# A state space scan as one scan instruction on turned states, streamed in eight units, in place of 62 steps

## The chip, the cores and the metric

The kernel runs on one core of a Trainium2 chip. It is one launch of an encoder layer on two sequences. The metric is the device time of one execution in microseconds (us). A core has five engines that work at the same time from queues of their own: PE (TensorE, matmuls; PEld is its weight load), DVE (VectorE), ACT (ScalarE), POOL (GpSimd) and SP (SyncE, which issues nearly all DMAs here). Instructions of one engine run in the order of its queue; between engines they wait on semaphores. All data is fp32; gate and projection matmuls take each operand as a high and a low part (fp32r), so that one product is three matmuls.

## The reference, cut to what matters

The layer norms the input `x` (512 tokens, width 1024, two sequences), projects it by `w_in`, and has three branches: a state space branch (S5), a differential attention and a cross attention to a memory. They are gated, summed, projected, and a feed-forward network follows. The change touches the S5 branch alone:

```python
def _ssm_combine(e1, e2):
    a1, b1 = e1
    a2, b2 = e2
    return a1 * a2, a2 * b1 + b2

def _s5_scan_dir(u, lam, step, b, c):
    lam_bar = jnp.exp(lam * step[:, None])
    b_bar = ((lam_bar - 1.0) / lam)[..., None] * b
    bu = jnp.einsum('lgh,gph->lgp', u.astype(jnp.complex64), b_bar)
    a = jnp.broadcast_to(lam_bar, bu.shape)
    _, xs = lax.associative_scan(_ssm_combine, (a, bu), axis=0)
    return jnp.real(jnp.einsum('lgp,ghp->lgh', xs, c))
```

There are 32 groups (`g`) of 16 channels (`h`) and 64 complex states (`p`), and two directions over the tokens, whose outputs are summed. A gelu and a gated linear unit (glu) follow: `z * sigmoid(z @ w_glu + b_glu)`.

## The kernel before, in words

Tokens are cut into 64 chunks (`NC`) of 8 (`T`). Inside a chunk the recurrence is written out as matmuls; across chunks a state per group has to be carried on. Partitions 0 to 63 hold the states of the forward direction and 64 to 127 those of the backward one, so a state tile is 128 partitions x real or imaginary x 32 groups x 2 sequences x 64 chunks.

`s5_gen` (from L1468) is a Python generator. Whenever the program calls `next(s5)`, the next part of the branch is written into the instruction stream; between the calls stands other work. In order it does this:

- constants: from lambda and step it works out powers of the complex decay (L1489 to L1563), small DVE instructions of 128x32;
- `input_weights(o)` for each of four blocks `o` of eight groups (L1615): six DVE products of 128x1024 (L1609 to L1611), transposes on PE (L1623), copies by ACT (L1624), kept in SBUF (`wb`);
- `output_weights(o)` (L1638): six more such products, two copies on POOL (L1640, L1641), small matmuls for the kernels inside a chunk (L1656; two at a time, with outputs at partitions 0 and 64), all stored to DRAM (`cD`, `gD5`);
- states: `u` is loaded back from DRAM into one tile (L1674); 64 matmuls of 128x128 weights and 128 columns (L1687) give each chunk's input to the state; ACT and DVE copy them into the state tile `st` (L1690, L1691);
- the scan across chunks: 62 steps of four DVE instructions on 128x128 (L1702 to L1705), a complex multiply and add;
- outputs: for each block copies of the states (L1738, L1739), 96 matmuls (three for each group, L1746 to L1748), copies by ACT, stores to `yD` (L1753). The gelu stage (L501 to L512) reads `yD`, and its results `zh`, `zl` are the moving operands of the glu projections (L524).

The other work that fills the time between is `gates(n)` (L400): each gate is a projection of 48 matmuls of 128x128 by 512 columns (L66 is the line of a helper that records every matmul), with a weight tile loaded by SP (L146), cast to its high part by ACT (L134, `wh`) and its low part by DVE (L135, `wl`), two buffers of each, and a tanh on ACT (L408). `NG` says how many gates stand where: `NG[0]` before the scan, `NG[1]` less some along it, one at each of the scan's places in `SCAN` but the first, two among the outputs, and `NG[2]` after the gelu stage. That is 7, 2, 4, 2 and 3.

A scheduler gives each engine its order: it walks the program as written, simulates the engines' times, and puts an instruction on its queue when it would be ready, those written earlier first. `tc.issue_after(x)` makes instructions of `x`'s engine in the block stand behind `x` on that engine. The scan's parts are held behind the split of the last gate's weight (`last_s[1]` is the `wl` on DVE), the outputs behind the last gate's last matmul.

Pools hold the tiles in SBUF. A pool that closes gives its memory to the next, which waits for the instructions that still use it: the state tile takes the memory that the constants leave.

Of the kernel before, what the change touches and what calls it, by code (L numbers as in the profile page):

```python
# [10 lines left out]
F32 = mybir.dt.float32  # L11
# [30 lines left out]
NG = (7, 6, 3)  # L42
# [3 lines left out]
SCAN = (33, 40, 47, 53, 60)  # L46
# [26 lines left out]
def encoder(ctx: ExitStack, tc: tile.TileContext, a, out):  # L73
# [339 lines left out]
    next(s5)  # L413
    gates(NG[1] + 1 - len(SCAN))
    for i in range(len(SCAN)):
        if i:
            gates(1)
        with tc.issue_after(last_s[1].ins):
            next(s5)
    for n in (0, 1, 1):  # L420
        gates(n)
        with behind():
            next(s5)
    next(s5, None)

# [1042 lines left out]
def s5_gen(k):  # L1468
# [3 lines left out]
    st, pre, rt = ExitStack(), ExitStack(), ExitStack()  # L1472
    k.open_tags(st, su=1)
    sp = st.enter_context(tc.tile_pool(name="s5", bufs=1, reuse_waits="tile"))
    cp = rt.enter_context(tc.tile_pool(name="s5c", bufs=1, side="right", reuse_waits="tile"))
    V.memset(cp.tile([P, 64], F32, name="pad_s"), 0.0)
    k.open_tags(rt, side="right", it=3, wb=6)
# [86 lines left out]

    yield
# [48 lines left out]

    def input_weights(o):  # L1615
        res = []
        for w_ in cprod("it", by_group(b_r, o), by_group(b_i, o), by_token(qr, o), by_token(qi, o), True):
# [7 lines left out]
            res.append(t_)  # L1625
        return res

    wbs = [input_weights(o) for o in range(3)]
# [39 lines left out]
    output_weights(0)  # L1668
    output_weights(1)
    uv = k.uD.rearrange("(g h) j s c -> j h g (s c)", h=16)  # L1670
    u_ = slot("su", [P, G, NS * NC], name="u_")
    for o in range(4):
        for j in range(8):
            nc.sync.dma_start(u_[j * 16 : (j + 1) * 16, 8 * o : 8 * o + 8], uv[j, :, 8 * o : 8 * o + 8])  # L1674


    pre.close()
    ss = st.enter_context(tc.tile_pool(name="s5s", bufs=1, reuse_waits="tile"))
    st_t = ss.tile([P, 2, G, NS, NC], F32, name="st")
    PO.memset(st_t[:, :, :, :, 0:1], 0.0)  # L1680
    for o in range(4):
        for ri, w_ in enumerate(wbs[o]):
            for g4 in range(2):
                ps = aux()
                for g in range(4):
                    gg = g4 * 4 + g
                    PE.matmul(ps[:, g * P : (g + 1) * P], w_[:, gg * P : (gg + 1) * P], u_[:, 8 * o + gg, :], start=True, stop=True)  # L1687
                pv = ps.rearrange("p (q c) -> p q c", c=NC)
                dv = st_t[:, ri, 8 * o + 4 * g4 : 8 * o + 4 * g4 + 4].rearrange("p g s c -> p (g s) c")
                S.copy(dv[0:64, :, 1:NC], pv[0:64, :, 0 : NC - 1])  # L1690
                V.tensor_copy(dv[64:128, :, NC - 1 : 0 : -1], pv[64:128, :, 1:NC])  # L1691
        if o == 0:
            wbs.append(input_weights(3))
    for o in range(2, 4):
        output_weights(o)
    yield
    sv = st_t.rearrange("p r g s c -> p r (g s) c")
    l8rv, l8iv = l8r.rearrange("p r g s -> p r (g s)"), l8i.rearrange("p r g s -> p r (g s)")
    for i in range(2, NC):
# [8 lines left out]
    yield  # L1708

    rt.close()  # L1710
    k.open_tags(rt, side="right", x2=2, oc=4, ow=3, sy=2)
# [141 lines left out]
```

## Time and profile before

| what | value |
|---|---|
| runs | 1588.4 and 1587.11 us, median 1587.76 us |
| profiled execution, span from first to last instruction | 1585.2 us (no other time is given for it) |
| PE busy | 99% of the span |
| DVE, ACT, POOL busy | 74%, 40%, 35% |
| DMA moved | 237.84 MB, mean 150 GB/s |
| first and last instruction of the 62 scan steps | 148.4 to about 254 us |
| last store of the branch's output issued | 317.4 us |
| glu projection begins | 345 us |

The profile is one execution, recorded by the hardware. Busy time is the time in which at least one instruction of an engine ran. Matmuls overlap in the pipeline, so a matmul's duration is not its price: the time from one start to the next is. A group row gives line, engine, operation, output and inputs by name, shapes, count, then busy us and mean ns of one, then the engine's idle time just before such instructions and what ended it. A row of one line or tile gives the least, median and greatest duration in ns and the first and last start in us. The profiler counts an fp32 matmul as two records, each with a weight load of its own.

### The profile page before, as it was taken

The page shows a single profiled execution, that of the slowest core. Times are in us where ns is not written, and L with a number is a line of the kernel's source. Part 1 is how long each engine was busy: PE and PEld are TensorE (multiplying, and loading weights), DVE is VectorE, ACT ScalarE, POOL GpSimd, SP SyncE. Part 2 cuts the span into 40 slices and gives each one's busy share as a digit, 9 for nine tenths or more (in the row PEclk, how much of TensorE's full clock was granted, in tenths as well). Part 3 has the DMA queues.
Part 4 walks back from the last instruction along what each step waited for, and adds up shares of the span by engine and source line. Part 5 has one row for each costly group of instructions (what it writes and reads, how often), then busy time and mean ns, then how long its engine had stood idle before and what let it go on. Part 6 is the DMA issues. An engine that isn't in the chain of part 4 may idle for free. (4 is left out here: it accounts for less than half of the span.)

```text
span 1585.2 us, 21351 instructions
## 1 busy us (share of the span) xinstructions
PE 1574.0 (99%) x7738; PEld 1310.4 (83%) x7738; DVE 1170.4 (74%) x1859; ACT 631.6 (40%) x1115; POOL 549.5 (35%) x434
## 2 busy tenths in 40 slices
PE   9999999999999999999999999999999999999998
PEld 7888888888898779778888888888888888888777
DVE  7978995076774776866545669788888877988864
ACT  6644223265552455564223443333333333233323
POOL 0010000001333321300343355767777553444663
PEclk9999999999999999999999999999999999999999
DMA  9553623676763121135544422333333323885412
GB/s 363 183 170 119 212 94 116 180 266 204 269 218 113 41 100 41 47 127 174 198 140 128 137 93 93 112 107 120 120 120 125 118 84 128 306 324 184 160 61 107
DMA packets 105675, 237.84 MB, mean 150 GB/s; under 512 B 13665, under 2 KB 45409, under 8 KB 105569
## 3 DMA queue, kind: packets, MB, share of 16 engines
q1 hardware_dynamic: 104992, 236.06, 44.2%
q8 instruction: 61, 1.00, 0.3%
q14 instruction: 46, 0.37, 0.1%
q10 hardware_dynamic: 576, 0.41, 0.1%
HBM read 165.16 MB, written 71.27 MB: 149 GB/s over the span
## 5 line engine op out<-in xcount | busy, mean ns | idle before, releaser
L66 PE MATMUL bkmm<-xh,wh 128*128 128x512 f32 x640 | 255.3, 399 | 0.0
L66 PE MATMUL bkmm<-xh,wl 128*128 128x512 f32 x640 | 250.6, 392 | 0.0
L66 PE MATMUL bkmm<-xl,wh 128*128 128x512 f32 x640 | 250.1, 391 | 0.0
L66 PE MATMUL bkmm<-tl,wh 128*128 128x512 f32 (+1 forms) x621 | 241.1, 388 | 0.0
L66 PE MATMUL bkmm<-th,wl 128*128 128x512 f32 (+1 forms) x621 | 240.7, 388 | 0.0
L66 PE MATMUL bkmm<-th,wh 128*128 128x512 f32 (+1 forms) x621 | 240.7, 388 | 0.0
L134 ACT CAST wh<-wf 128x1024 fp32r<-128x1024 f32 (+2 forms) x134 | 117.6, 878 | 261.2 <-PE bkmm L66 190.4
L135 DVE TENSOR_TENSOR wl<-wf,wh 128x1024 fp32r<-128x1024 f32 (+2 forms) x134 | 147.6, 1102 | 60.5 <-ACT wh L134 55.4
L66 PE MATMUL bkmm<-th,w 128*128 128x512 f32 x432 | 140.7, 391 | 1.9 <-DVE nsq L1112 1.2
L66 PEld LDWEIGHTS bkmm<-xh,wh 128*128 128x128 f32 x640 | 120.3, 188 | 26.2 <-issue 3.4
L66 PEld LDWEIGHTS bkmm<-xh,wl 128*128 128x128 f32 x640 | 120.2, 188 | 26.2 <-issue 0.4
L66 PEld LDWEIGHTS bkmm<-xl,wh 128*128 128x128 f32 x640 | 120.4, 188 | 22.3
L66 PEld LDWEIGHTS bkmm<-th,wh 128*128 128x128 f32 x621 | 116.6, 188 | 24.0
L66 PEld LDWEIGHTS bkmm<-th,wl 128*128 128x128 f32 x621 | 116.5, 188 | 24.1 <-DVE wl L135 0.2
L66 PEld LDWEIGHTS bkmm<-tl,wh 128*128 128x128 f32 x621 | 116.6, 188 | 23.8
L1175 POOL TENSOR_TENSOR up<-up,acc 128x512 f32<-128x512 f32 x44 | 83.7, 1920 | 90.6 <-DVE up L1112 86.8
L452 POOL TENSOR_TENSOR raw<-raw 128x128 f32<-128x128 f32 x28 | 14.6, 523 | 288.9 <-DVE nb L543 231.9
L66 PEld LDWEIGHTS bkmm<-th,w 128*128 128x128 f32 x432 | 80.9, 188 | 22.1 <-DVE nsq L1112 2.1
L792 POOL TENSOR_TENSOR mg<-mg,gl 128x1024 f32<-128x1024 f32 x16 | 43.8, 2740 | 136.8 <-DVE gl L788 132.1
L66 PE MATMUL bkmm<-tl,w 128*128 128x512 f32 x216 | 84.1, 389 | 0.0
L134 ACT CAST wh<-ws 128x1024 fp32r<-128x1024 f32 x44 | 46.3, 1052 | 91.3 <-PE bkmm L66 49.7
L66 PE MATMUL bkmm<-yh,wh 128*128 128x512 f32 x192 | 76.2, 397 | 0.0
(663 smaller groups left out, 3535.4 us busy)
## 6 DMA issues: line engine op xcount, KB each, us to landing
wf<-in_w_in SPq DMA_DIRECT2D x40, 512.0 KB, 3.9
wD<-hl SPq DMA_DIRECT2D x28, 512.0 KB, 2.9
w<-wD SPq DMA_DIRECT2D x28, 512.0 KB, 4.8
gD<-gt SPq DMA_DIRECT2D x24, 512.0 KB, 2.9
gl<-gD SPq DMA_DIRECT2D x24, 512.0 KB, 3.7
wf<-in_w_fg SPq DMA_DIRECT2D x22, 512.0 KB, 3.6
wf<-in_w_fu SPq DMA_DIRECT2D x22, 512.0 KB, 3.5
aD<-ac SPq DMA_DIRECT2D x22, 512.0 KB, 2.8
```

Of the source, the lines that this page charges most:

```text
L66: return self.put(self.eng.matmul(*args, **kw))
L134: h = S.copy(hi, src)
L135: l_ = V.tensor_tensor(out=lo, in0=src, in1=hi.bitcast(F32), op=ALU.subtract)
L452: PO.tensor_tensor(out=a22, in0=a21, in1=a22, op=ALU.add)
L792: PO.tensor_tensor(out=mg[m], in0=mg[m], in1=gt, op=ALU.add)
L1175: PO.tensor_tensor(out=up, in0=up, in1=accs[s], op=ALU.mult)
```

## The change

The decay is taken apart into its size and its phase. If each state is turned back by the phase of its chunk, what is left is a real recurrence with a constant real factor, and real and imaginary parts run on their own. After it the states are turned forward again. One new DVE instruction, `tensor_tensor_scan`, does a whole real recurrence: 512 elements for four groups, two sequences and 64 chunks, where a zero in front of each sequence's first chunk stops the carry.

- New constants: `wc`, `ws` (the phase over eight tokens) and `r8` (the size), 22 small DVE instructions before the first input weights; `l8r` and `l8i` go.
- A table `tab` of the phases of 64 chunks for 32 groups, made on POOL by doubling (36 instructions of 32 to 992 elements), stored to DRAM (`tD5`).
- `input_weights` stores its result to DRAM (`bD5`) and all four blocks come before the units.
- The states, scan and outputs become eight units of four groups. `unit_in(q)` loads `u`, weights and a piece of the table; `states(q)` does 16 matmuls with half of the columns each (64 wide, 126 moving columns, at output partitions 0 and 64, those of the second half reading the chunks in reverse), turns the states (four multiplies on DVE that read PSUM, two adds on POOL) and runs two scans; `outputs(q)` turns them back (four multiplies on DVE, adds by halves on DVE and POOL) and does the 12 matmuls of four groups as before.
- `output_weights(o)` moves to the units, one every second unit. Unit `q`'s states stand with unit `q-1`'s outputs in one step of the generator.
- Gates: two before, one after each of the nine steps, four after them, three after the gelu stage.

The diff, cut:

```diff
-NG = (7, 6, 3)
+NG = (2, 4, 3)
...
-SCAN = (33, 40, 47, 53, 60)
...
     next(s5)
     gates(NG[0])
-    next(s5)
-    gates(NG[1] + 1 - len(SCAN))
-    for i in range(len(SCAN)):
-        if i:
-            gates(1)
+    for _ in range(9):
         with tc.issue_after(last_s[1].ins):
             next(s5)
-    for n in (0, 1, 1):
-        gates(n)
-        with behind():
-            next(s5)
+        gates(1)
     next(s5, None)
+    gates(NG[1])
...
+    rot = sp.tile([P, 8, G], F32, name="rot")
...
+    wc, ws, r8, ra = (rot[:, i, :] for i in range(4))
+    q1, q2 = ta[:, :G], tb[:, :G]
+    V.tensor_scalar(out=ra, in0=E, scalar1=1.0, scalar2=None, op0=ALU.add)
+    V.tensor_tensor(out=r8, in0=ra, in1=ra, op=ALU.mult)
+    V.tensor_tensor(out=ra, in0=r8, in1=r8, op=ALU.mult)
+    V.tensor_tensor(out=r8, in0=ra, in1=ra, op=ALU.mult)
+    c_, s_ = cp1, sn
+    for _ in range(3):
+        V.tensor_tensor(out=q1, in0=c_, in1=c_, op=ALU.mult)
+        V.tensor_tensor(out=q2, in0=s_, in1=s_, op=ALU.mult)
+        V.scalar_tensor_tensor(out=ws, in0=c_, scalar=2.0, in1=s_, op0=ALU.mult, op1=ALU.mult)
+        V.tensor_tensor(out=wc, in0=q1, in1=q2, op=ALU.subtract)
+        c_, s_ = wc, ws
+    V.tensor_tensor(out=q1, in0=wc, in1=wc, op=ALU.mult)
+    V.tensor_tensor(out=q2, in0=ws, in1=ws, op=ALU.mult)
+    V.tensor_tensor(out=q1, in0=q1, in1=q2, op=ALU.add)
+    V.tensor_scalar(out=q1, in0=q1, scalar1=-0.5, scalar2=1.5, op0=ALU.mult, op1=ALU.add)
+    V.tensor_tensor(out=wc, in0=wc, in1=q1, op=ALU.mult)
+    V.tensor_tensor(out=ws, in0=ws, in1=q1, op=ALU.mult)
...
-    l8r = sp.tile([P, 2, G, NS], F32, name="l8r")
-    l8i = sp.tile([P, 2, G, NS], F32, name="l8i")
-    for s in range(NS):
-        for ri in range(2):
-            S.copy(l8r[:, ri, :, s], pr[:, 8, :])
-        S.mul(l8i[:, 0, :, s], pi[:, 8, :], -1.0)
-        S.copy(l8i[:, 1, :, s], pi[:, 8, :])
...
+    bD = drp.tile([4, P, 2, 8 * P], F32, name="bD5")
...
+            nc.sync.dma_start(bD[o, :, ri], t_)
...
+    input_weights(3)
+    wt.close()
+    pre.close()
+    tD = drp.tile([8, P, 2, 4, NC], F32, name="tD5")
+    with tc.tile_pool(name="s5t", bufs=1, reuse_waits="tile") as tp:
+        tab = tp.tile([P, 2, G, NC], F32, name="tab")
+        u1, u2 = (tp.tile([P, G, NC // 2], F32, name=n_) for n_ in ("tu1", "tu2"))
+        PO.memset(tab[:, 0, :, 0:1], 1.0)
+        PO.memset(tab[:, 1, :, 0:1], 0.0)
+        for ri, w_ in enumerate((wc, ws)):
+            PO.tensor_copy(tab[:, ri, :, 1], w_)
+        n = 1
+        while n < NC - 1:
+            m = min(n, NC - 1 - n)
+            hi = [tab[:, ri, :, n : n + 1].broadcast_to([P, G, m]) for ri in range(2)]
+            lo = [tab[:, ri, :, 1 : m + 1] for ri in range(2)]
+            cmul(PO, tab[:, 0, :, n + 1 : n + 1 + m], tab[:, 1, :, n + 1 : n + 1 + m], *hi, *lo, u1[:, :, :m], u2[:, :, :m])
+            n += m
+        for q in range(8):
+            nc.sync.dma_start(tD[q], tab[:, :, 4 * q : 4 * q + 4])
+    k.open_tags(st, z5=1, uu=2, bw=2, tb=2, ow=2, oc=2, sy=2, tm=4, x2=2)
+    zt = slot("z5", [P, 2, 3, 4, NS, NC], name="zt5")
+    PO.memset(zt.rearrange("p a r g s c -> p (a r g s) c")[:, :, 0:1], 0.0)
...
+    def unit_in(q):
+        o, h4 = q // 2, q % 2
+        if h4 == 0:
+            us[o] = slot("uu", [P, 8, NS * NC], name="u_")
+            for j in range(8):
+                nc.sync.dma_start(us[o][j * 16 : (j + 1) * 16], uv[j, :, 8 * o : 8 * o + 8])
+        bw = slot("bw", [P, 2, 4 * P], name="bw")
+        nc.sync.dma_start(bw, bD[o, :, :, 512 * h4 : 512 * h4 + 512])
+        tb = slot("tb", [P, 2, 4, NC], name="tb")
+        nc.sync.dma_start(tb, tD[q])
+        ins[q] = bw, tb
+    def states(q):
+        o, h4 = q // 2, q % 2
+        bw, tb = ins[q]
+        z = zt[:, q % 2]
+        S.copy(z[:, 2, :, :, 1:], r8[:, 4 * q : 4 * q + 4].unsqueeze(2).unsqueeze(3).broadcast_to([P, 4, NS, NC - 1]))
+        bk = [aux() for _ in range(2)]
+        for g in range(4):
+            ug = us[o][:, 4 * h4 + g].rearrange("p (s c) -> p s c", s=NS)
+            for ri in range(2):
+                for hf, u_ in enumerate((ug[:, :, 0 : NC - 1], ug[:, :, NC - 1 : 0 : -1])):
+                    d_ = bk[ri][64 * hf : 64 * hf + 64, g * P : (g + 1) * P].rearrange("p (s c) -> p s c", s=NS)
+                    tc.keep_in_program_order(
+                        PE.matmul(d_[:, :, 1:], bw[:, ri, g * P + 64 * hf : g * P + 64 * hf + 64], u_, start=True, stop=True))
+        bk = [b_.rearrange("p (g s c) -> p g s c", g=4, s=NS)[:, :, :, 1:] for b_ in bk]
+        cs, sn_ = (tb[:, i, :, 1:].unsqueeze(2).broadcast_to([P, 4, NS, NC - 1]) for i in range(2))
+        for i, op in enumerate((ALU.add, ALU.subtract)):
+            t_ = slot("tm", [P, 4, NS, NC], name="tm")
+            V.tensor_tensor(out=z[:, i, :, :, 1:], in0=bk[i], in1=cs, op=ALU.mult)
+            V.tensor_tensor(out=t_[:, :, :, 1:], in0=bk[1 - i], in1=sn_, op=ALU.mult)
+            PO.tensor_tensor(out=z[:, i, :, :, 1:], in0=z[:, i, :, :, 1:], in1=t_[:, :, :, 1:], op=op)
+        for i in range(2):
+            zf = z[:, i].rearrange("p g s c -> p (g s c)")
+            V.tensor_tensor_scan(out=zf, data0=z[:, 2].rearrange("p g s c -> p (g s c)"), data1=zf, initial=0.0,
+                                 op0=ALU.mult, op1=ALU.add)
+    def outputs(q):
+        o, h4 = q // 2, q % 2
+        _, tb = ins.pop(q)
+        z = zt[:, q % 2]
+        if h4 == 0:
+            w_ = slot("ow", [P, 8, P], name="w_")
+            gv = gD[8 * o : 8 * o + 8].rearrange("g h t q -> h g (t q)")
+            for j in range(8):
+                nc.sync.dma_start(w_[j * 16 : (j + 1) * 16], gv[:, :, (7 - j) * 16 : (7 - j) * 16 + 128])
+            ys[o] = w_, slot("sy", [P, 8, P], name="y_")
+        w_, y_ = ys[o]
+        cc = slot("oc", [P, 2, 4, P], name="cc")
+        for ri in range(2):
+            nc.sync.dma_start(cc[:, ri], cD[o, ri, :, 4 * h4 : 4 * h4 + 4, 0:P])
+        x2 = slot("x2", [P, 2, 4 * NS, NC], name="x2")
+        sh = [P, 4, NS, NC]
+        cs, sn_ = (tb[:, i].unsqueeze(2).broadcast_to(sh) for i in range(2))
+        for i, op in enumerate((ALU.subtract, ALU.add)):
+            t1, t2 = (slot("tm", sh, name="tm") for _ in range(2))
+            V.tensor_tensor(out=t1, in0=z[:, i], in1=cs, op=ALU.mult)
+            V.tensor_tensor(out=t2, in0=z[:, 1 - i], in1=sn_, op=ALU.mult)
+            t1, t2 = (t_.rearrange("p g s c -> p (g s) c") for t_ in (t1, t2))
+            V.tensor_tensor(out=x2[0:64, i], in0=t1[0:64], in1=t2[0:64], op=op)
+            PO.tensor_tensor(out=x2[64:128, i, :, ::-1], in0=t1[64:128], in1=t2[64:128], op=op)
+        ps = aux()
+        for g in range(4):
+            d_ = ps[:, g * P : (g + 1) * P]
+            PE.matmul(d_, w_[:, 4 * h4 + g, :], us[o][:, 4 * h4 + g, :], start=True, stop=False)
+            for ri in range(2):
+                PE.matmul(d_, cc[:, ri, g], x2[:, ri, 2 * g : 2 * g + 2, :].rearrange("p s c -> p (s c)"), start=False, stop=(ri == 1))
+        S.copy(y_[:, 4 * h4 : 4 * h4 + 4, :].rearrange("p g c -> p (g c)"), ps)
+        if h4:
+            for j in range(8):
+                nc.sync.dma_start(yv[j, :, 8 * o : 8 * o + 8], y_[j * 16 : (j + 1) * 16])
+    unit_in(0)
...
-    for i in range(2, NC):
-        p_ = sp.tile([P, 2, G * NS], F32, tag="p_", name="p_")
-        q_ = sp.tile([P, 2, G * NS], F32, tag="q_", name="q_")
-        V.tensor_tensor(out=p_, in0=sv[:, :, :, i - 1], in1=l8rv, op=ALU.mult)
-        V.tensor_tensor(out=q_, in0=sv[:, ::-1, :, i - 1], in1=l8iv, op=ALU.mult)
-        V.tensor_tensor(out=p_, in0=p_, in1=sv[:, :, :, i], op=ALU.add)
-        V.tensor_tensor(out=sv[:, :, :, i], in0=p_, in1=q_, op=ALU.add)
-        if i in SCAN:
-            yield
...
+    for q in range(9):
+        if q % 2 == 0 and q < 8:
+            output_weights(q // 2)
+        if q + 1 < 8:
+            unit_in(q + 1)
+        if q < 8:
+            states(q)
+        if q:
+            outputs(q - 1)
+        yield
```

More of the change, by code (lines that the diff above doesn't have):

```diff
@@ L1612, in cprod @@
         return tiles
+    bD = drp.tile([4, P, 2, 8 * P], F32, name="bD5")
     def input_weights(o):
-        res = []
-        for w_ in cprod("it", by_group(b_r, o), by_group(b_i, o), by_token(qr, o), by_token(qi, o), True):
+        for ri, w_ in enumerate(cprod("it", by_group(b_r, o), by_group(b_i, o), by_token(qr, o), by_token(qi, o), True)):
             w_ = w_.rearrange("p g e h -> p (g e h)")
@@ L1624, in input_weights @@
                 S.copy(t_[:, g4 * 512 : g4 * 512 + 512], tr)
-            res.append(t_)
-        return res
-    wbs = [input_weights(o) for o in range(3)]
+            nc.sync.dma_start(bD[o, :, ri], t_)
+    for o in range(3):
+        input_weights(o)
     yield
@@ L1666, in output_weights @@
                 nc.sync.dma_start(gv[:, :, 112:128], gk[r0 + 32 : r0 + 48, :, 128:144])
-    output_weights(0)
-    output_weights(1)
-    uv = k.uD.rearrange("(g h) j s c -> j h g (s c)", h=16)
[L1671 to L1693, printed above, removed]
```

57 lines of the change are left out of this document (6 added, 51 removed).

## The prediction

> **What bounds the kernel now.** I read the page's head first, then the busy time of each engine by stage, then the matrix engine's instructions in order of time through the stretch that the change touches.
>
> ```profile
> span 1585.2 us, 21351 instructions
> PE 1574.0 (99%) x7738; PEld 1310.4 (83%) x7738; DVE 1170.4 (74%) x1859; ACT 631.6 (40%) x1115; POOL 549.5 (35%) x434
> ```
>
> A busy matmul row may hide slack, so the stages count for more. The columns are busy us and instruction counts of PE, weight load, DVE, ACT, POOL, then granted clock, DMA share, GB/s.
>
> ```profile
> 95.00:150.00 55.00, 55.00 (x374) 47.78 (x374) 42.86 (x47) 27.45 (x53) 4.92 (x5) 1.00 0.55 175
> 150.00:255.00 105.00, 105.00 (x500) 86.82 (x497) 98.59 (x259) 25.53 (x43) 0.58 (x2) 1.00 0.41 137
> 255.00:315.00 60.00, 60.00 (x364) 53.33 (x363) 9.05 (x8) 19.30 (x23) 0.00 (x0) 1.00 0.49 149
> 315.00:350.00 35.00, 35.00 (x156) 28.99 (x155) 26.03 (x48) 20.76 (x30) 0.00 (x0) 1.00 0.75 259
> ```
>
> From 95 to 350 us PE is never idle and its clock is at 1.00. The scan with its 248 small DVE instructions lies in 150:255, where DVE is busy 98.59 of 105 us, and PE runs gate projections all that time. So DVE is nearly full there and still off the path. Whether a busy PE also advances is seen from its starts (time, duration, then the instruction):
>
> ```profile
> 102.40 0.39 PE L66 MATMUL bkmm<-xh,wh 128*128 128x512 f32 x1
> 102.62 0.39 PE L66 MATMUL bkmm<-xl,wh 128*128 128x512 f32 x1
> 102.94 0.45 PE L1656 MATMUL bktr<-cxi,l 128*48 128x144 f32 x4
> 103.23 0.42 PE L1656 MATMUL bktr<-cxr,l 128*48 128x144 f32 x4
> ...
> 104.70 0.42 PE L1656 MATMUL bktr<-cxr,l 128*48 128x144 f32 x4
> 105.04 0.50 PE L66 MATMUL bkmm<-xh,wl 128*128 128x512 f32 x1
> 105.38 0.39 PE L66 MATMUL bkmm<-xh,wh 128*128 128x512 f32 x1
> ...
> 117.79 2.05 PE L1687 MATMUL bktr<-u__1192,wb 128*128 128x128 f32 x16
> 119.60 0.48 PE L66 MATMUL bkmm<-xh,wh 128*128 128x512 f32 x1
> 119.92 1.05 PE L1687 MATMUL bktr<-u__1192,wb 128*128 128x128 f32 x8
> ```
>
> Gate matmuls start every 0.227 us (the 0.39 us are overlapping lives), which makes a gate of 48 of them 10.9 us. Nothing waits between them. **The consequence**: in this stretch PE sets the end. A shorter scan gives nothing back by itself. The change can gain only what it takes off PE's own list of matmuls, and can lose what it adds to that list or whatever makes PE stand still.
>
> **The sum, PE's list first.** Against the profiled execution (span 1585.2 us; no other time of it is given) the two timed runs lie 1.9 and 3.2 us higher, the median 1587.76 lies 2.6 higher. I add 2.6 to every sum.
>
> Gates: 7+2+4+2 stand before the gelu stage now, 2+9+4 after the change, and 3 behind in both. Eighteen gates stay, at 10.9 us each; they only change places. Transposes of the input weights, kernel matmuls of L1656 and the 96 output matmuls stay in number.
>
> State matmuls: now 64 full 128x128 ones, two records each; 16 records take 1.81 us (117.79 to 119.60), so 0.113 a record, 0.226 a matmul, 14.5 us in all. After: 64 pairs, each pair filling columns 0 to 63 and 64 to 127 with 126 moving columns. A pair of half-width fp32 matmuls has a row: in L1656 a line of x4 is two matmuls with outputs at partitions 0 and 64, and 8 such lines take 2.10 us (102.94 to 105.04, the change-over at the end included). That is 0.245 us a pair net of 0.1 for that change-over, while one matmul of 144 columns by itself would need 0.25 (0.226 x 144/128). So the two halves run at the same time. With 126 columns a pair costs 0.215 (0.245 x 126/144) to 0.245. 64 pairs: 13.8 to 15.7 us, against 14.5: **-0.7 to +1.2, I take 0**. Reversed and two-piece moving operands have no row; the lower bound is the same -0.7 and the upper that the halves queue, 14.5 more (a rival).
>
> Change-overs: from gate to another kind and back the starts are 0.32 and 0.34 apart in place of 0.227, about 0.1 each. L1687 shows the same 0.32 (119.60 to 119.92) without halves. Now about 8 stretches of L1687 and 8 of outputs; then 8 of states and 8 of outputs, or a few more: 0 to +2 us, **I take +0.5**.
>
> The rows on weight loads (ns min, median, max):
>
> ```profile
> L1656 PEld LDWEIGHTS bktr<-cxi,l x64: 119/123/123, 102.9 to 164.0; 128*48 128x48 f32 x64
> L1687 PEld LDWEIGHTS bktr<-u__1192,wb x128: 186/192/192, 117.8 to 146.6; 128*128 128x128 f32 x128
> ```
>
> Half-width loads are shorter, not longer, and they are hidden in the pair's 0.245. [...]
>
> **Early DVE work.** 22 instructions on 128x32 for the rotation and radius are added before the input weights. Their row, and the tightest place that they push:
>
> ```profile
> L1500 DVE SCALAR_TENSOR_TENSOR E<-E 128x32 f32<-128x32 f32 x7 | 1.4, 194 | 0.0
> ```
>
> ```profile
> 57.42 1.22 DVE L135 TENSOR_TENSOR wl<-wf,wh 128x1024 fp32r<-128x1024 f32 x1
> ```
>
> ```profile
> 58.90 0.39 PE L66 MATMUL bkmm<-xh,wh 128*128 128x512 f32 x1
> ```
>
> 22 x 0.2 = 4.4 us on a DVE that is nearly full from 25 to 60 us. The split that ends at 58.64 is used by the third matmul after 58.90, near 59.4, so its cover is 0.7 us. If all 4.4 us land ahead of it PE loses 3.7; if they fall in gaps, 0. There are gaps (the chain of small instructions can be put anywhere before the table needs it), **so +1.0**.
>
> **The units.** Prices on DVE and POOL:
>
> ```profile
> L1611 DVE TENSOR_TENSOR cxi<-ct,cxi 128x1024 f32<-128x1024 f32 x8 | 9.8, 1222 | 0.2
> ```
>
> ```profile
> L1112 DVE TENSOR_TENSOR up<-bkmm,u x56: 676/683/694, 953.9 to 1532.4; 128x512 f32<-128x512 f32 x56
> ```
>
> ```profile
> L135 DVE TENSOR_TENSOR tl<-fa,th x9: 686/1774/1784, 1342.4 to 1472.1; 128x512 fp32r<-128x512 f32 x9
> ```
>
> ```profile
> L792 POOL TENSOR_TENSOR mg<-mg,gl 128x1024 f32<-128x1024 f32 x16 | 43.8, 2740 | 136.8 <-DVE gl L788 132.1 <-issue 4.7
> L182 POOL TENSOR_TENSOR acc<-acc,nsq 128x512 f32<-128x512 f32 x20 | 29.0, 1450 | 58.2 <-ACT nsq L181 58.2
> L182 POOL TENSOR_TENSOR acc<-acc,nsq 128x256 f32<-128x256 f32 x10 | 7.4, 741 | 14.3 <-ACT nsq L181 14.1
> L452 POOL TENSOR_TENSOR raw<-raw 128x128 f32<-128x128 f32 x28 | 14.6, 523 | 288.9 <-DVE nb L543 231.9 <-DVE hl L138 52.1 <-DMA raw<-in_w_fo 4.9
> ```
>
> *Table on POOL:* six rounds of six instructions on 32, 64, 128, 256, 512 and 992 elements. From the rows 0.52, 0.74, 1.45 and 2.66 for the last four, and 0.3 and 0.4 by continuing them downward: 6.1 x 6 = 36 us.
>
> *One unit on DVE:* four multiplies that read PSUM at 0.68 (L1112), six from SBUF at 0.69, and two scans of 512. A scan has no row. It is bounded by the plain 512-element form at 0.69 and by twice that, 1.4; I take 1.0. Sum 2.7 + 4.1 + 2.0 = 8.8 us. Half of an output-weight block (six of 1.22, so 3.7) and a gate's split (1.2) come with it: 13.7. *On POOL:* four at 1.45, 5.8. *On PE:* 8 pairs 1.8, 12 outputs 2.7, half a kernel block 1.0, a gate 10.9: 16.4. So PE is the slowest of the three in each unit, and the 105 us of scan give way to 8 x 8.8 = 70 us of DVE, spread.
>
> Do DVE and POOL disturb each other? L135 on 512 elements from SBUF takes 0.69 at best and 1.77 in the median in a stretch where POOL works, while L1112, with one input from PSUM, stays at 0.68 to 0.69. So the two take turns where DVE has two SBUF inputs. Taking turns, a unit needs 5.8 + 13.7 - 2.7 = 16.8 us, level with PE. [...]
>
> *When does it end?* The S5 result is due at these rows:
>
> ```profile
> L1753 SPq DMA_DIRECT2D yD<-y__2954 x8: 326/431/572, 314.0 to 317.4; - x8
> ```
>
> ```profile
> L66 PEld LDWEIGHTS bkmm<-zh,wh x32: 187/188/192, 345.0 to 366.6; 128*128 128x128 f32 x32
> L137 ACT ACTIVATE zh<-zy x8: 614/617/634, 330.7 to 347.6; 128x512 fp32r<-128x512 f32 x8
> ```
>
> Now the last y store is issued at 317.4 and PE takes the first zh at 345 with no pause; the stage holds the same 18 gates after the change, so 317 remains about the due time. The table can start when its memory comes free, at the place of today's memset:
>
> ```profile
> 65.85 0.34 POOL L1680 MEMSET st<- 128x128 f32 x1 [64.38 <-DVE b_i L1542]
> ```
>
> ```profile
> gD<-gt SPq DMA_DIRECT2D x24, 512.0 KB, 2.9
> ```
>
> 66 + 36 = 102 if POOL runs freely, 146 if each of its 36 instructions lets one of 1.22 on DVE go first; plus 6 for the table's way out and back (2.9 twice): 108 to 152. Eight units of 16.8 and some 10 for the last outputs: 252 to 296. That is ahead of 317, so the gelu stage isn't late. All of the S5 work is then covered by gates, and I cost it at nothing; without that cover it costs PE one us per us behind 317.
>
> *Waits behind which something queues:* a unit's multiplies wait on DVE for the table, and the next gate's split is queued behind them; on SP the table's stores wait for POOL, and gate weights are queued behind. Today's margin of a split:
>
> ```profile
> 201.83 1.22 DVE L135 TENSOR_TENSOR wl<-wf,wh 128x1024 fp32r<-128x1024 f32 x1
> ```
>
> ```profile
> 205.03 0.59 ACT L408 ACTIVATE gt<-bkmm 128x512 f32<-128x512 f32 x1
> ```
>
> The split is done at 203.05, and the gate that needs it begins as the one before is read out at 205.0: 2 us in this place. A unit's chain stands a few us now and then; 0 if the order suits, up to 9 us (about one each), **I take +1.5**.
>
> The DMA added (input weights, table: some 12 MB both ways, against 237.84 MB in the whole) lies in stages at 0.41 to 0.55 of DMA time and hides there. Sum: 1585.2 + 2.6 + 0 + 0.5 + 1.0 + 1.5 = **1590.8 us**.
>
> **The rivals.**
> *Slower: the table holds up the queues.* Place: first unit's multiplies on DVE, the table's stores on SP. Taking turns with DVE, the table is ready at 152 in place of 108. It decides from the point at which DVE stands longer than the gates already split reach, one gate of 10.9 us. Price up to 44 - 11 = 33 us, more likely half, 17. Time 1608, at worst 1624. For: the 1.77 us rows. Against: DVE is slowed by the same turns, so it comes late to that wait. Chance 0.12, of which 0.06 over 2%.
> *The halves don't overlap* (strided or reversed operands, or gates put between): +14.5, 1605. Against: L1656. Chance 0.07.
> *The units end after 317*: at 20 us each from 152, 152 + 160 + 10 = 322, +5, 1596; needs scans near 2.5 us. Chance 0.08.
> *Faster by over 2%*: needs 32 us less on PE, and the change takes at most 0.7 off it. Chance 0.01.
>
> **How the numbers follow.** The forecast (no measurable change, 1590.8, own range 1586 to 1596) has 0.72. The range takes the lower bound of the sum and two of the rivals in: 1585 to 1608. Two per cent, about what a measurement of this kernel can tell from no change, is 1556 to 1619.5. Slower by more: 0.06 from the table and 0.01 from the others together; faster 0.01; within 0.92.
>
> **What would show it.** Right: PE busy all through 95 to 350 us, gates 10.9 us apart, states pairs of 0.22 to 0.25 us, DVE well below its 98.59 of 105 us, POOL some 36 us busy from about 66, last y store before 317, first zh taken near 345 to 350. Wrong: PE idle of over 10 us in front of a wl or a table, half-width matmuls one after the other, a last y store past 320, or a total outside the range with PE full, which would mean that PE's list has other prices than these.

## The result and the profile after

The changed kernel takes **1644.75 us** (1643.35 and 1646.15) against 1587.76: 1.036 of the time before, 95% interval 1.033 to 1.039. It is slower by 57 us, where no measurable change was forecast, and it lies outside the range.

The head of the page of the changed kernel:

```profile
span 1644.4 us, 21634 instructions
PE 1594.3 (97%) x7866; PEld 1321.6 (80%) x7866; DVE 1184.7 (72%) x1709; ACT 619.5 (38%) x1095; POOL 665.0 (40%) x506
```

The same stages as the prediction showed of before, with the same columns:

```profile
95.00:150.00 55.00, 37.36 (x185) 30.25 (x183) 36.80 (x17) 16.25 (x30) 31.98 (x16) 0.86 0.38 138
150.00:255.00 105.00, 89.23 (x563) 73.66 (x564) 75.05 (x76) 21.84 (x43) 37.21 (x24) 0.90 0.66 205
255.00:315.00 60.00, 55.61 (x360) 46.95 (x361) 46.31 (x67) 10.96 (x18) 24.89 (x14) 0.97 0.58 168
315.00:350.00 35.00, 35.00 (x154) 29.33 (x154) 24.27 (x26) 18.21 (x25) 0.00 (x0) 0.95 0.55 194
sum 255.00, PE 217.20 PEld 180.19 DVE 182.44 ACT 67.25 POOL 94.08; mean PE 54.30 PEld 45.05 DVE 45.61 ACT 16.81 POOL 23.52
```

PE, full for all 255 us before, is idle for 37.8 of them (255 less 217.20), and its clock, 1.00 before, is 0.86 and 0.90 where most of the idle time lies. DVE has indeed become lighter in 150:255, 75.05 in place of 98.59, and the kernel gained nothing by it.

All of the loss lies ahead of the glu projection. These are rows of the tile `zh` in the changed kernel:

```profile
L65 PE MATMUL bkmm<-zh,wh x32: 388/389/398, 404.0 to 425.6; 128*128 128x512 f32 x32
L136 ACT ACTIVATE zh<-zy x8: 617/620/633, 329.3 to 343.3; 128x512 fp32r<-128x512 f32 x8
```

PE comes to the glu at 404.0, before at 345.3: 58.7 us later, and the spans differ by 59.2. Its operand `zh` was made at the usual time (329 to 343, before 331 to 348). So the branch's result is not late. PE is late, because it stood still on the way and still had its gates to do.

Where it stood, from the waits of PE, the largest ones (us in all, times, longest):

```profile
PE bktr L1731 <- DMA cD<-cxr: 10.8, 1, 10.8
PE bktr L1771 <- DMA w__1551<-gD: 9.4, 1, 9.4
PE bktr L1665 <- POOL cxi L1650: 6.9, 1, 6.9
PE bktr L1773 <- POOL x L1767: 5.6, 3, 3.1
```

The three long ones (by PE's starts at 131, 141 and 170 us) come one after the other: the first kernel matmuls, the first state matmuls, the first output matmuls. Each stands in PE's queue ahead of gates, and each waits for data of the first unit. The name behind the wait of 10.8 us isn't what its matmuls need: the view names the semaphore that came last. The state matmuls read `u` and `bw`, and `bw` was loaded from 147.3 on, as SP's rows below show; the store `cD` is nothing that they read. Why nearly all of that is late stands on SP. Its instructions in order of time (start, duration):

```profile
81.28 9.15 SPq L1634 DMA_DIRECT2D bD<-wb  x3
126.04 0.62 SPq L1698 DMA_DIRECT2D tD<-tab  x1
...
127.35 4.15 SPq L1698 DMA_DIRECT2D tD<-tab  x6
...
132.27 0.40 SPq L391 DMA_DIRECT2D uD<-ut  x1
...
135.78 0.44 SPq L145 DMA_DIRECT2D wf<-in_w_in  x1
...
140.06 6.53 SPq L1712 DMA_DIRECT2D u__1227<-uD  x7
147.31 0.58 SPq L1714 DMA_DIRECT2D bw<-bD  x1
```

and its wait, as the view of waits has it:

```profile
SPq L1698 <- POOL tab L1537: 35.1, 1, 35.1
```

From 90.9 to 126.0 SP issues nothing: the first store of the table is at the head of its queue, and the table isn't ready. Behind it stand the stores of `u` (`uD`), a gate's weight (`wf`), the stores of the input weights (`bD`) and the loads of the first unit (`u`, `bw`). Of these only the first unit's loads have anything to do with the first unit's table. From 127 on they all go out in one heap.

SP isn't the only queue that the late table stops. The units' tile `zt` takes the memory that the table's pool leaves, so its first writers wait until the stores have read the table. On ACT that is a copy that stands for 26.0 us, on POOL a memset that stands for 10.4:

```profile
ACT zt L1723 <- DMA tD<-tab: 26.0, 1, 26.0
137.59 0.18 POOL L1702 MEMSET zt<- 128x48 f32 x1 [10.35 <-DMA tD<-tab]
```

Right behind that memset POOL's copy `cxi` (L1650) starts, at 137.67, and the first of PE's three long waits ends with it. No run has the late table without this reuse of memory.

The table itself, first and last instructions on POOL in order of time, 36 of them, one behind the other from 64.39 to 126.02:

```profile
64.39 0.72 POOL L1532 TENSOR_TENSOR tu<-tab 128x32 f32<-128x32 f32 x1
...
122.82 3.20 POOL L1537 TENSOR_TENSOR tab<-tu,tu 128x992 f32<-128x992 f32 x1
```

and DVE in the same time:

```profile
109.06 2.92 DVE L134 TENSOR_TENSOR wl<-wf,wh 128x1024 fp32r<-128x1024 f32 x1
...
123.86 3.24 DVE L1618 TENSOR_TENSOR cxi<-cr,xi__742 128x1024 f32<-128x1024 f32 x1
127.13 1.23 DVE L1619 TENSOR_TENSOR cxi<-ct,cxi 128x1024 f32<-128x1024 f32 x1
```

The two engines go one for one, at the end with 3.2 and 3.2 us, and the first DVE instruction after the table's end takes 1.23 again.

**The clock.** After its second long wait, of 10.8 us, PE doesn't go on at full speed. A window of 10 us of the changed kernel, in which that wait ends (at 152.51):

```profile
150.00:160.00 10.00, 7.49 (x45) 6.47 (x46) 3.03 (x4) 0.00 (x0) 1.36 (x1) 0.59 0.91 310
```

PE works for 7.49 us of it, and the window's mean granted clock is 0.59. Its gate matmuls start 0.43 us apart at 156.66 to 157.94, and 0.23 apart behind 158.28.

**The account of the 58.8 us**, by PE's starts up to its first glu matmul (my own sum over all intervals from one start to the next, each against the usual step of its kind; the number of gate matmuls is the same in both kernels):

| | before | after | difference |
|---|---|---|---|
| usual steps of the whole list | 336.9 | 337.7 | +0.8 |
| intervals longer than usual by over 0.5 us | 1.1 | 41.8 | +40.7 |
| other excess: half clock, change-overs | 6.1 | 23.4 | +17.3 |

Of the last row, change-overs between kinds of matmul make 2.7 us (73 of them after 85 us, for 37). The rest, 14.6, I put down to the clock. The trace bears that out: over the six stretches in which it has the granted clock at 0.50 (44.4 us together), PE works for 27.3 us; with gate steps of 0.43 us there for 0.227 it loses about half of that, an estimate of 13.6.

### The profile page after: what moved, and what is told of

It is laid out like the page before. It is cut to its first block, busy times and chain, and to the rows that moved or that the text cites. A ratio compares the mean times of both kernels' runs of the same rounds, so it can differ in the third digit from the quotient of the medians.

```text
span 1644.4 us, 21634 instructions
## 1 busy us (share of the span) xinstructions
PE 1594.3 (97%) x7866; PEld 1321.6 (80%) x7866; DVE 1184.7 (72%) x1709; ACT 619.5 (38%) x1095; POOL 665.0 (40%) x506
## 5 line engine op out<-in xcount | busy, mean ns | idle before, releaser
L65 PEld LDWEIGHTS bkmm<-th,wh 128*128 128x128 f32 x621 | 116.6, 188 | 23.8
L746 POOL TENSOR_TENSOR t<-t,rs 128x512 f32<-128x512 f32 x16 | 26.9, 1682 | 137.4 <-DVE t L745 137.4
```

The source lines that it names most:

```text
L65: return self.put(self.eng.matmul(*args, **kw))
L746: PO.tensor_tensor(out=t2, in0=t2, in1=rope[1], op=ALU.mult)
```

## The experiments

My theory, **A**: the loss is the table's stores at the head of SP's queue, which make everything behind them late, and PE's own queue, which has the unit's matmuls ahead of gates. Rivals: the units themselves are too slow (POOL's adds, DVE's turns), or PE's list costs more than before. All runs below were timed together with the kernel before on the same chip (medians 1587.65, 1587.74 and 1587.66 us for the runs in `x`, `y` and `z`). In all the same 18 gates are computed.

| run | what is different from the changed kernel | us | ratio to before, 95% |
|---|---|---|---|
| `x1_table_dve` | table made on DVE | 1616.0 | 1.016 to 1.019 |
| `x2_table_filled` | table filled, no doubling | 1608.05 | 1.010 to 1.014 |
| `x3_store_late` | table on POOL, its stores written two gates later | 1619.07 | 1.018 to 1.021 |
| `x4_gates_first` | gates 6, 9, 0 for 2, 9, 4 | 1620.96 | 1.019 to 1.022 |
| `y1_filled_adds_dve` | table filled, units' adds on DVE | 1597.96 | 1.005 to 1.008 |
| `y2_all_dve` | table and adds on DVE | 1604.85 | 1.010 to 1.013 |
| `y3_all_dve_gates_first` | the same, gates 6, 9, 0 | 1597.0 | 1.005 to 1.008 |
| `y4_late_and_first` | stores late and six gates first | 1612.39 | 1.014 to 1.017 |
| `z1_filled_gates_first` | table filled, adds on DVE, gates 6, 9, 0 | 1596.41 | 1.004 to 1.007 |
| `z2_table_behind_stores` | table filled and stored, doubling run behind the stores | 1627.32 | 1.024 to 1.027 |

**The table on DVE.**

```diff
-            PO.tensor_copy(tab[:, ri, :, 1], w_)
+            V.tensor_copy(tab[:, ri, :, 1], w_)
...
-            cmul(PO, tab[:, 0, :, n + 1 : n + 1 + m], ...
+            cmul(V, tab[:, 0, :, n + 1 : n + 1 + m], ...
```

> The 36 table instructions go from POOL to DVE, all else as in the changed kernel. Theory A (the SP queue stands 35.1 us for the table's last POOL instruction, with gate weights, u stores and input weights queued behind it): the table takes some 18 us of DVE and no turns with POOL, SP's wait for the table falls under 8 us, PE's gaps over 0.5 us fall from 40 us to under 12, time 1590 to 1602. Theory B (the loss lies in the units: scans, POOL adds and states placed too early in PE's list): the waits in the units stay, time at least 1615.

1616.0: half of the loss is gone (28.8 of 57). That is less than A said, and it lies inside what B named (at least 1615). The table is hardly earlier. What changed is where its stores stand in SP's order. Rows of SP in this run:

```profile
98.58 0.32 SPq L391 DMA_DIRECT2D uD<-ut  x1
99.74 0.33 SPq L145 DMA_DIRECT2D wf<-in_w_in  x1
...
121.79 5.69 SPq L1698 DMA_DIRECT2D tD<-tab  x8
```

The table's stores go out at 121.8, only 4.3 us ahead of the changed kernel's, but now a store of `u` and a gate's weight went out long before them, at 98.6 and 99.7. So it isn't the table's own time that made the difference. What is queued behind it did, or the turns: with POOL out of the way DVE's 128x1024 instructions take 1.2 us in this run, and this run alone doesn't part the two. The scheduler puts an instruction in the queue where it believes that it will be ready, and the place at which SP met them in the changed kernel, 90.9, says that it believed POOL's table ready about then (this is argued from the order; no run shows the scheduler's own times). What is left of the loss has another place; the waits of PE in this run:

```profile
PE bktr L1773 <- POOL x L1767: 11.7, 5, 4.7
PE bktr L1731 <- DMA bw<-bD: 3.7, 1, 3.7
```

**The table filled.**

```diff
-        n = 1
-        while n < NC - 1:
...
+        for ri in range(2):
+            PO.memset(tab[:, ri, :, 2:], 1.0 - ri)
```

> The doubling is left out: the table is filled with ones and zeros by two memsets, so states are not turned rightly, and every later instruction stays. Theory A: the table's stores find their data ready, no SP wait for POOL over 5 us, time 1588 to 1600. Theory B: at least 1615. If it is faster than the kernel with the table on DVE by over 5 us, the table's 18 us on DVE cost PE something too.

1608.05, between the two ranges and so a miss for both. Without any doubling, its turns and the waits for it 36.7 us of the 57 are gone and 20.3 remain, so the table isn't the whole cause. The largest waits of PE are now in the units, first of all three on POOL's half adds:

```profile
PE bktr L1768 <- POOL x L1762: 5.6, 3, 3.1
```

**The stores later, the table as it is.** A `yield` is put ahead of the stores, and the part behind it is written after gate 4, held behind that gate's weight load on SP.

```diff
-NG = (2, 4, 3)
+NG = (4, 2, 3)
...
     gates(NG[0])
+    with queued():
+        next(s5)
...
+        yield
         for q in range(8):
             nc.sync.dma_start(tD[q], tab[:, :, 4 * q : 4 * q + 4])
```

> The table stays on POOL with all its turns against DVE; only its stores and the first unit's loads stand behind the weight load of the fourth gate on SP in place of the second (gates 4, 9, 2 in place of 2, 9, 4). Theory A: uD stores, input-weight stores and two more gate weights pass ahead of the table, SP stands for it under 12 us, time 1592 to 1608. Theory C (POOL and DVE taking turns slows the weight splits, and that is what starves PE): the turns are all still there, time stays over 1625.

1619.07: 25.7 us come back with POOL's table and all its turns untouched, fewer than A said and more than C allowed. SP's wait shrinks from 35.1 us to

```profile
SPq L1701 <- POOL tab L1539: 9.3, 1, 9.3
```

Two gates are moved ahead in this run too, so it isn't the queue alone.

**Gates first, the queue as it is.** `NG = (6, 0, 3)`, nothing else.

> Gates 6, 9, 0 in place of 2, 9, 4: four more gates stand ahead of the units in the program and so in PE's list, while the table's stores keep their place on SP (two gate weights ahead of them). Theory A: SP stands as long as before, the gates that PE would run have no weights, time 1630 to 1650. Theory B' (PE's own list puts kernel and state matmuls ahead of gates that could run): the gates fill PE, time at most 1608.

1620.96, between the two, a miss for both. SP stands nearly as long as before, and still 23.8 us come back:

```profile
SPq L1698 <- POOL tab L1537: 31.6, 1, 31.6
```

So the late queue cost PE here only what PE had nothing else to do for. Four more gates are 43.6 us of such work, but they don't hide all of it, because their weights stand in the same queue (SP loads the next one at 131.6):

```profile
PE bkmm L65 <- ACT wh L133: 7.2, 1, 7.2
```

**Stores late and gates first.**

```diff
-NG = (2, 4, 3)
+NG = (4, 0, 3)
...
     gates(NG[0])
+    with queued():
+        next(s5)
+    gates(2)
```

> Table and adds on POOL as in the changed kernel; the table's stores stand behind the fourth gate's weight on SP, and six gates stand ahead of the units. If the blocked SP queue and PE's list are two losses, the gains of 25.7 and 23.8 us add until the units' own loss is left: 1604 to 1612. If they repair one and the same loss: 1615 to 1621.

1612.39, 32.4 us back, where the two alone gave 25.7 and 23.8; just above the one range and below the other. It doesn't settle whether these are two losses or one: only 36.7 us hang on the table (the run with the filled one), so 25.7 and 23.8 couldn't have added up in any case. But beside the run before, this one gives the cleanest comparison for SP's queue. Six gates stand ahead of the units in both, and only the place of the stores, and of what is written behind them, differs. SP's wait falls from 31.6 us to

```profile
SPq L1702 <- POOL tab L1540: 9.4, 1, 9.4
```

and 8.6 us come back (1620.96 to 1612.39). The 25.7 of the run with the late stores hold the two gates as well, and can't be put down to SP alone.

**POOL's adds in the units.** `PO.tensor_tensor` becomes `V.tensor_tensor` in the 16 adds of the states and the 16 half adds of the outputs, in the kernel with the filled table:

> The table is filled as in the run before (1608.05 us; states not turned rightly), and the units' 32 adds on POOL go to DVE. Theory D (what is left is POOL: its adds take 1.5 and 2.0 us and take turns with DVE, so outputs come later than the order of the queues assumed): the gaps of PE in the units fall from about 10 us to under 4, time 1597 to 1603. Theory E (PE's list has no gate between states and outputs, and DVE's own chain of scan and multiplies is late): the gaps stay at 8 us or more, time 1605 to 1612.

1597.96, 10.1 us less than with the adds on POOL, as expected. This is a second loss, of its own. DVE gains on it too: with the adds on DVE and six gates first (the run `z1_filled_gates_first` below) the multiply that turns the states back takes 0.68 us,

```profile
L1759 DVE TENSOR_TENSOR tm<-zt,tb x16: 665/678/685, 191.2 to 308.4; 128x512 f32<-128x512 f32 x16
```

while in the changed kernel, beside POOL, the same multiply (L1764) has a median of 1.20 us. Its row there, and the scan's:

```profile
L1741 DVE TENSOR_TENSOR_SCAN zt<-zt x16: 1205/1210/2307, 163.0 to 302.2; 128x512 f32<-128x512 f32 x16
L1764 DVE TENSOR_TENSOR tm<-zt,tb x16: 654/1204/1784, 173.5 to 309.1; 128x512 f32<-128x512 f32 x16
```

**Everything on DVE**, table and adds:

> Table and adds all on DVE, the whole computation, gates 2, 9, 4. Theory D: from 1616.0 with the table alone on DVE down to 1598 to 1607. Theory E: 1611 to 1618.

1604.85, as expected: a real table costs 6.9 us more than a filled one even on DVE. With `NG = (6, 0, 3)` besides:

> The same with gates 6, 9, 0. Theory B' (PE's list puts state and output matmuls ahead of gates that could run while the first units' data are still on their way): the waits for bw and the first outputs, 4 and 5 us with the table on DVE, go, time 2 to 9 us under the kernel with all on DVE. If only POOL's lateness matters, it is the same within 2 us. Neither should beat the kernel before, because PE's list is 0.8 us longer and has some 36 more changes of kind, 2.7 us.

1597.0, as expected. This is the best version that computes the whole branch. It takes back 47.8 of the 57 us and doesn't beat the kernel before.

**What is left without both losses**: table filled, adds on DVE, gates 6, 9, 0.

> The changed kernel with the table filled by two memsets (the doubling is left out, so the states are not turned rightly), the units' 32 POOL adds on DVE, and six gate tiles ahead of the fifth stage's list in place of two (6, 0, 3 for 2, 4, 3). It asks what the change costs when neither loss is there. With the table on DVE that order took 7.9 us off (1604.85 to 1597.0). Theory D (the two losses and PE's list order explain all; what is left is the longer list, +0.8, the change-overs, +2.7, and the early DVE work, about 1): 1590 to 1595. Rival F (the change has a price beyond these that no order takes away): 1596 to 1600, with gaps in front of PE still over 5 us in all.

1596.41, just above D's range and inside F's, while the gaps (4.6 us more than before, by PE's starts) are a little under what F named, so neither holds in full. The stages of this run:

```profile
95.00:150.00 55.00, 55.00 (x259) 45.86 (x257) 12.04 (x11) 16.16 (x24) 1.32 (x1) 1.00 0.43 155
150.00:255.00 105.00, 103.74 (x683) 86.30 (x681) 84.02 (x100) 29.59 (x60) 6.69 (x7) 1.00 0.61 191
255.00:315.00 60.00, 58.57 (x389) 49.68 (x390) 47.47 (x85) 12.11 (x21) 0.00 (x0) 1.00 0.64 192
```

PE is nearly full again and its clock is 1.00. To the glu it needs 9.4 us more than before: 0.8 of list, 4.6 of gaps in the units, 1.0 in gate steps, 3.0 of other excess, mostly change-overs. So the new form of the scan has a price of some 9 us here even without the two losses.

**The doubling behind the stores**, meant to show the turns of POOL and DVE without the queue:

```diff
+        for ri in range(2):
+            PO.memset(tab[:, ri, :, 2:], 1.0 - ri)
         for q in range(8):
             nc.sync.dma_start(tD[q], tab[:, :, 4 * q : 4 * q + 4])
+        n = 1
+        while n < NC - 1:
...
```

> The table filled by two memsets and stored, as in the run at 1608.05, and then the whole doubling run on POOL behind the stores, its result unused (so the states are not turned rightly). POOL's 36 instructions and their turns with DVE are there, but nothing on SP waits for them. It tells the queue from the turns. Theory A (the queue behind the table's stores is the loss; the turns alone matter little): 1608 to 1617, and the wait of the stores on POOL is gone from SP. Rival T (DVE slowed by the turns makes the unit's inputs late by itself, queue or no queue): 1628 to 1645, with gaps of PE over 25 us. Between the two, the turns have that share.

1627.32, between the two, and it doesn't tell them apart, because the waits came back at other places. The stores no longer wait, but the units' tiles take the memory of the closed pool, which POOL still uses. On SP the first load of `u` waits for that:

```profile
SPq L1714 <- POOL zt L1704: 19.1, 1, 19.1
```

And on ACT a copy into `zt` waits for it, with the cast of a gate's weight behind it, until the doubling's last instruction ends at 123.6:

```profile
123.65 1.12 ACT L1725 COPY zt<-rot 128x504 f32<-128x504 f32 x2 [24.25 <-POOL tab L1537]
124.67 1.04 ACT L133 CAST wh<-wf 128x1024 fp32r<-128x1024 f32 x1
```

That weight had long been there (SP issues no load of one between 104.4 and 139), and the largest of PE's waits, which ends at 125.8, is for this cast:

```profile
PE bkmm L65 <- ACT wh L133: 8.9, 1, 8.9
```

So this run cost 19.3 us more than the filled table by the same sort of wait, in the queues of SP and ACT. Beside that it shows two prices of POOL's instructions in one stream. The shorter ones I read as those without DVE beside it (DVE is busy for 25.86 of the 55 us of 95:150 in this run):

```profile
85.10 1.28 POOL L1532 TENSOR_TENSOR tu<-tab 128x128 f32<-128x128 f32 x1
86.33 0.42 POOL L1533 TENSOR_TENSOR tu<-tab 128x128 f32<-128x128 f32 x1
...
105.35 2.15 POOL L1534 TENSOR_TENSOR tab<-tu,tu 128x512 f32<-128x512 f32 x1
107.57 1.12 POOL L1535 TENSOR_TENSOR tu<-tab 128x512 f32<-128x512 f32 x1
```

How much the turns cost by themselves has no run of its own. One piece can be seen: PE's wait of 2.4 us at 107 is for a gate's split (`wl`) that took DVE 2.12 us beside POOL, and with the table on DVE or filled no wait of PE for a split is over 0.7. An estimate: the run with the stores late and the gates first has the table on POOL with all its turns, at 1612.4; the one with filled table, adds on DVE and gates first, at 1596.4, with the 10.1 us of POOL's adds put on top, gives 1606.5. Some 6 us are then for the turns and what is left of SP's wait (9.4 us in that run).

## Why the prediction was wrong, point by point

**What held.** *A shorter scan gives nothing back by itself*: in the run without both losses PE is nearly full, DVE works 84.02 us of 150:255 in place of 98.59, and the kernel is still 8.8 us slower than before. *The state matmuls, -0.7 to +1.2*: where they run at full clock in the changed kernel, seven pairs (28 records) start at 276.14 and the next kind at 277.80,

```profile
276.14 1.73 PE L1731 MATMUL bktr<-u__2167,bw 128*64 128x126 f32 x28
277.80 0.49 PE L1771 MATMUL bktr<-u__1838,w__2209 128*128 128x128 f32 x2
```

0.237 a pair, 15.2 us for 64 against 14.5: +0.7. So the halves overlap, and that rival is out. *A table ready between 108 and 152*: it was ready at 126, and SP loaded it back from 134.

**Half right.** *The gelu stage isn't late*: `zh` was there in time, but the units weren't on theirs. Their last multiply starts at 309, where their end was put at 252 to 296, and the last y store goes out at 323.4, past the 317 that I had as due and past the 320 that I had named as a sign of being wrong. It cost nothing because PE was later still.

**Terms mis-sized.** Change-overs: +2.7 for +0.5, above the upper bound of 2, since states and outputs are cut into more stretches (73 changes for 37). The scan: 1.21 us for 1.0, inside its bounds, of which the upper one, twice the plain form, was my estimate and no row's. Together they are 2 to 3 us, of no weight beside the rest. One reading was off: the first matmul on the split that ends at 58.64 starts at 59.80 and not near 59.4, so its cover was 1.2 us and not 0.7; nothing hung on it.

**The step that failed** is "All of the S5 work is then covered by gates, and I cost it at nothing", with "*Waits behind which something queues* [...] I take +1.5". I asked when the units would *end*, found 296 against 317, and took the stretch as covered. But cover has to hold at each point of each queue. The sentence ahead of it even says "on SP the table's stores wait for POOL, and gate weights are queued behind", and then it isn't priced. Its price was in reach: a table that is ready at 108 to 152 on one side, and on the other the place of its stores in SP's order, which is the scheduler's belief. By its own rule (an instruction is queued when it would be ready) a scheduler that counts no turns would place them long before 126; that it counts none is argued, not shown. SP stood from 90.9 to 126.0, and the intervals in which PE stood make 40.7 of the 58.8 us, where I had 0 for the covered work and 1.5 for waits. Four things that I left out came on top:

- what is behind the head of the queue is not only the unit's: stores of `u`, input weights, and gate weights all stood there;
- the tile that takes the table's memory waits for the stores as well, on ACT and on POOL. I asked when the table's own memory comes free, not who waits for the table's;
- PE has a queue too. Kernel, state and output matmuls of the first unit stood ahead of the gates, and PE waited 6.9, 10.8 and 9.4 us for them. In the first of these waits there was no gate to run, since SP had loaded no weight between 80 and 135.8. In the other two there was: DVE's splits of two gates were done at 144.4 and 147.0. Six gates ahead of the units give 23.8 us back with nearly the same SP wait;
- after most of its longer pauses PE ran at half its clock: some 14 us, 13.6 by the stretches at 0.50 and 14.6 by PE's starts (17.3 less 2.7 of change-overs).

**The rival that came true** was *the table holds up the queues*, in the right place ("the table's stores on SP"), given 0.12. Its price, 33 at most, was 24 too low, since it let a wait cost only its length beyond one gate of cover, on DVE. Its counter-argument ("DVE is slowed by the same turns, so it comes late to that wait") was about the wrong queue: SP was at its wait at 90.9 and stood there for 35.1 us. The second loss, 10 us for POOL's adds in the units, was in the sum as "0 if the order suits, up to 9 us", of which I took 1.5; the turns there were worked out as 16.8 us a unit, "level with PE", and that should have been read as no cover at all.

**What stays open**: how much of the 57 us the turns of POOL and DVE cost by slowing DVE alone (about 6 by the estimate above; the run that was to show it moved the wait instead), what the reuse of the table's memory costs apart from SP's queue, and how the remaining 9 us in the run without both losses divide in detail.

## What to carry to other kernels

Work that is moved to an idle engine was not free here, because a queue of another engine waited for its result (SP stood 35.1 us for POOL's table): ask for each queue when it arrives at the wait and what stands behind it, not when the work as a whole is due. The planned order decides where that wait stands, so work that is ready later than the order supposes (here POOL's table beside DVE, 61.6 us) blocks what stands behind it on that queue and has nothing to do with it (here stores of `u` and of input weights, and a gate's weight, from 90.9 to 126.0). Ask the same of memory: the first writers of the tile that took the table's place waited for its last readers, 26.0 us on ACT and 10.4 on POOL, with all that stood behind them. Where PE is full, ask what stands ahead of the waiting matmul in PE's own list (six gates there gave 23.8 us back, with SP's wait still at 31.6), and what the change takes off that list: here it took nothing off, and the best version of the whole branch stayed 9.3 us above the kernel before.

## What the runs showed of the hardware

**POOL and DVE in turns.** With two SBUF inputs on both sides the engines went one for one for 60 us: 36 instructions of POOL from 64.39 to 126.02 in the changed kernel, 37 of DVE. DVE's 128x1024 instructions, 1.23 us alone, took 1.4 to 1.7 beside POOL's of 128x256 and 2.9 to 3.35 beside those of 128x992. The units' 32 multiplies with one input from PSUM (L1736, L1737) all took 0.67 to 0.68, also the one at 161.11 that ran beside POOL's adds. A 128x128 copy of POOL took 0.29 at 137.67, where DVE ran nothing, and 1.36 at 156.99 beside DVE's 128x1024. In the run with the doubling behind the stores POOL's 128x512 instruction took 2.15 and 1.12, and its 128x128 one 1.28 and 0.42. So of these two the small one suffers more: the 128x128 one takes three times its shorter time, as long as one of DVE, the 128x512 one 1.9 times.

**The clock after a pause.** The pause need not be long. In the changed kernel one of 2.4 us is followed by gate steps of 0.59 and 0.43 us in place of 0.227:

```profile
106.97 0.80 PE L65 MATMUL bkmm<-xh,wl 128*128 128x512 f32 x1 [2.37 <-DVE wl L134]
107.56 0.63 PE L65 MATMUL bkmm<-xh,wh 128*128 128x512 f32 x1
107.99 0.63 PE L65 MATMUL bkmm<-xl,wh 128*128 128x512 f32 x1
```

The length alone doesn't decide. In the changed kernel a pause of 1.95 us is followed by 3.4 us at half clock (0.50 over 216.19 to 219.60), and one of 1.91 us leaves the granted clock at 1.00 (over 254.8 to 258):

```profile
216.19 0.76 PE L1773 MATMUL bktr<-x,cc 128*128 128x128 f32 x2 [1.95 <-DVE x L1766]
254.89 0.46 PE L1773 MATMUL bktr<-x,cc 128*128 128x128 f32 x2 [1.91 <-POOL x L1767]
```

A pause of 3.08 us that ends at 312.85 is followed by half clock up to 318.59 (0.50 over 311.76 to 318.59); in the run with the filled table one of 3.08 us leaves the clock at 1.00 (over 255 to 315):

```profile
276.56 0.49 PE L1768 MATMUL bktr<-x,cc 128*128 128x128 f32 x2 [3.08 <-POOL x L1762]
```

In the run without both losses the gaps in the units are 1.5 us and less, and the clock stays at 1.00 up to the glu. So 1.95 and 2.4 us were enough in their places, and 3.08 us did no harm in one.

**The scan instruction** takes 1.21 us for 512 elements in the changed kernel and 1.22 in the run without both losses (medians of 16), where a plain multiply of the same size takes 0.68 in the latter: a ratio of 1.8.
